# Weight tiles of a two-layer fp32 network placed by the address of the operand they meet, and one load moved to another queue

## The chip, the core and the metric

The kernel runs on one core of a Trainium2 chip. The metric is device time of one execution in microseconds (us). A core has TensorE (PE in the profile, with its weight loads shown apart as PEld), VectorE (DVE), ScalarE (ACT), GpSimd (POOL) and SyncE (SP), which here only issues DMAs. Operands lie in SBUF, 128 partitions side by side; an address below is the byte offset inside a partition.

## The reference

Two blocks of two layers each over x of 512 tokens by 1024 features, all in fp32, with a weight matrix behind nearly every step. Cut to its products:

```python
def first_block(x, c, ...):                      # i = 0: S5 state-space mixer, i = 1: short convolution
    for i in range(2):
        sh1, sc1, g1, sh2, sc2, g2 = split(silu(c) @ w_ada[i] + b_ada[i], 6)
        h = rms_norm(x, norm1_g[i]) * (1 + sc1) + sh1
        mix = s5_mixer(h, ...) if i == 0 else (bg * conv3(cg * v)) @ conv_w_out   # [bg, cg, v] = h @ conv_w_in
        x = x + g1 * mix
        h = rms_norm(x, norm2_g[i]) * (1 + sc2) + sh2
        g, u = split(h @ w_ffn_in[i], 2)
        x = x + g2 * ((silu(g) * u) @ w_ffn_out[i])
    return rms_norm(x, final_g)

def second_block(x, ...):                        # i = 0: dilated attention, i = 1: HGRN2
    for i in range(2):
        y = dilated_attention_mixer(x, ...) if i == 0 else hgrn2_mixer(x, ...)
        x = layer_norm(4 ** 0.25 * x + y, ln_mix_g[i], ln_mix_b[i])
        y = square(relu(x @ ffn_w_up[i])) @ ffn_w_down[i]
        x = layer_norm(4 ** 0.25 * x + y, ln_ffn_g[i], ln_ffn_b[i])
    return x
```

## The kernel before

**Products.** Activations are kept transposed, features on partitions and 512 tokens along the free axis. Each fp32 factor of a large product is split in two parts of type fp32r, a rounded one (`hi`) and the rest (`lo`), and a product is made of three: hi by hi, hi by lo, lo by hi. `mm` (L824 to L835) runs them for one block of 128 output features: for each of `nk` blocks of 128 input features three matmuls, L832, L833 and L834, whose stationary operand is a 128 by 128 piece of the weights (`whi`, `whi`, `wlo`) and whose moving operand is 512 or 256 columns of the activations (`hhi`, `hlo`, `hhi`). `mm_group` (L845 to L847) does the same for four output blocks at a time. The moving operands are `hhi`/`hlo` (the normalised input of a layer), `hidh`/`hidl` (its hidden values) and `ohi`/`olo` (the attention's output). Most products take 512 columns (`FULL`); where a layer's end waits on a norm, the tokens go in two halves of 256 (`HALF`). In a few products (the attention's and HGRN's `v`, L1205 and L1580, and the last product of all, L1734) the weights are the moving operand.

**Weights.** `load_raw` (L211) has SyncE load 1 MB of a weight matrix into one of three `raw` buffers. `split_w` (L781) takes a `whi` and a `wlo` buffer from the pool `wsp`, three of each, lets ScalarE write `whi` (L785) and VectorE `wlo` (L786). `load_centred` (L792) does so for matrices whose rows are made mean free. ScalarE may write a buffer again when TensorE has read it for the last time.

**Places.** In the built program the three `whi` and three `wlo` buffers are 8,192 bytes each, one behind the other, and start at 288 modulo 512. `hhi` and `hlo` start at 480 modulo 512, `hidh` and `hidl` at 288, but in the HGRN layer at 480; `ohi` and `olo` at 0. Every slice that a matmul reads starts a multiple of 512 bytes from its tile's start. By **distance** this text means the address of the weights of the next matmul less the address of the moving operand of the current one, modulo 512: it is 320 where `hhi` or `hlo` moves (288 - 480 + 512), 0 where `hidh` or `hidl` moves, but 320 in HGRN, and 288 where `ohi` or `olo` does.

**The start.** Ahead of these products stands the S5 mixer (`s5`, about the first 195 us), whose order is a list written by hand (`ORDER`), which a scheduler then lays out on each engine. ScalarE's queue issues constants, `brow`, `crow` and x in chunks (`xT`, L185, two DMAs of 1 MB in pieces of 512 bytes); SyncE's queue issues the small tables and then the adaptive-norm weights (`w_ada`, L232), 1 MB at a time. The chunks of x are first read by `token_scale` (L583). GpSimd builds the output tables `ft` (`out_tables`, L539 to L541).

Of the kernel before, what the change touches and what calls it, by code (L numbers as in the profile page):

```python
# [17 lines left out]
D = 1024  # L18
# [10 lines left out]
def make_consts():  # L29
# [30 lines left out]
    ct["selB"] = np.concatenate([(kj == 4 * (qi % 32) + r).astype(f) for r in range(4)], 1)  # L60
# [32 lines left out]
def body(ctx, tc, a, out):  # L93
# [100 lines left out]
    avg = const.tile([128, 128], F32, name="avg")  # L194
    P.memset(avg, 1.0 / D)
# [176 lines left out]
    def s5():  # L372
# [196 lines left out]
        def setup(_):  # L569

# [218 lines left out]
    def load(W, M, k0, nk, c0, ncol=256):  # L789
        return split_w(load_raw(W, k0, nk, c0, ncol, M), nk, ncol)  # L790

    def load_centred(W, M, k0, nk, nb, base=0):  # L792
# [20 lines left out]
    def centre(tag):  # L813
# [6 lines left out]
        T.matmul(mb, avg, z, start=True, stop=True)  # L820
# [30 lines left out]
    nxt, got = [], []  # L851

# [4 lines left out]
    def take(W, M, k0, nk, c0, ncol=256):  # L857
        return got.pop(0) if got else load(W, M, k0, nk, c0, ncol)
# [12 lines left out]
    def run(blocks, xh, xl, kx, nk, k0=0, first=0, halves=HALF, last=0, done=None):  # L871
# [9 lines left out]
        if last:  # L881
            ld = [load(W, M, k0, nk, c0) for W, M, c0, _ in blocks[end:]]
# [18 lines left out]
    def out_gemm(W, off, src, nkt, upd, done, centred=()):  # L901
# [5 lines left out]
        def part(c):  # L907
# [3 lines left out]
            if c in centred:  # L911
                ld = load_centred(W, D, k0, nk, 2)
                for m in range(0 if last else 8):
                    upd(m, mm(ld[m // 4], m % 4, xh, xl, kx, nk, FULL[0]), FULL[0], c, last)
            elif not last:
                for b in range(4):
                    w = load(W, D, k0, nk, b * 256)
                    for s in range(2):
                        upd(2 * b + s, mm(w, s, xh, xl, kx, nk, FULL[0]), FULL[0], c, last)
            else:  # L920
                ld = [load(W, D, k0, nk, b * 512, 512) for b in range(2)]
# [132 lines left out]
    def to_load(W, M, *cols):  # L1054
        nxt.extend([lambda c0=c0: load(W, M, 0, 8, c0) for c0 in cols])
# [72 lines left out]
    def qk_load(g, pr):  # L1128
# [15 lines left out]
    def upd_deep(ssum):  # L1144
        cnt = {}

        def upd(m, ps, ts, c, last):
# [7 lines left out]
            if last and ssum is not None:  # L1155
                accum_sq(ssum, m, ts, x)
# [11 lines left out]
    ap_ = at.enter_context(tc.tile_pool(name="at", bufs=2, reuse_waits="tile"))  # L1168
    load_consts(ap_, "m1", "selB", bufs=1)
# [22 lines left out]
    def v_items(g, b4):  # L1192
# [86 lines left out]
    def soft_steps(pr, steps, base):  # L1279
# [169 lines left out]
    got.append(load(Wa, DA, 0, 8, 2 * D))  # L1449
# [36 lines left out]
    w = load_centred(Wao, D, 6, 2, 1)[0]  # L1486
# [43 lines left out]
    hid_p = hg.enter_context(tc.tile_pool(name="hid3", bufs=1, reuse_waits="tile"))  # L1530
    inv_k = const.tile([128, 1], F32, name="inv_k")
# [21 lines left out]
    def hgrn_pair(b, first):  # L1553
# [20 lines left out]
        wv = load(Wh, 3 * D, 0, 8, 2 * D + b * 256)  # L1574
# [9 lines left out]
        for s in range(2):  # L1584
# [72 lines left out]
            for j in range(4):  # L1657
# [16 lines left out]
    psG = psum(mm=5, st=3)  # L1674
    part(1)
# [94 lines left out]
```

## Time and profile before

| | |
|---|---|
| three runs | 2798.68, 2799.27 and 2801.44 us, median 2799.27 |
| the profiled execution | 2796.92 us, its span 2795.1 us |
| TensorE busy | 2725.6 us, 98% of the span |
| VectorE, ScalarE, GpSimd busy | 56%, 38%, 5% |
| mean granted share of TensorE's clock | 0.992 |

A page of the profile gives busy times and the chain of work that ended last; groups of instructions give count and mean duration; a stretch gives each engine's busy time and count. A matmul's shown duration is longer than the distance between two starts, since matmuls overlap in TensorE's pipeline, so the pace is read from starts: the length of a stretch over the products that start in it.

### The profile page before, as it was taken

Reading aid. Unit: us, or ns where it says so; the run is one execution under the profiler, and the core shown is the slowest. Engines: PE = TensorE matmul, PEld = TensorE weight load, DVE = VectorE, ACT = ScalarE, POOL = GpSimd, SP = SyncE. Lnnn points to the kernel's source line nnn. Section 1 sums busy time; section 2 is a strip of 40 time slices with the busy share of each in tenths; the row PEclk is TensorE's granted clock in tenths of the full one; section 3 lists DMA queues with packets and bytes.
Section 4 is the critical chain, followed back from the end, with each engine's and each line's share of the span. In section 5 each row is a group of like instructions: output and inputs, shape, how many; then the busy total and the mean of one; then the engine's idle time right before and its main releaser. Section 6 shows DMA issues by size and latency. Waiting matters only on the chain.

```text
span 2795.1 us, 37486 instructions
## 1 busy us (share of the span) xinstructions
PE 2725.6 (98%) x15356; PEld 2282.9 (82%) x15356; DVE 1569.4 (56%) x2803; ACT 1068.5 (38%) x1874; POOL 127.2 (5%) x124
## 2 busy tenths in 40 slices
PE   5899999999999999999999999999999999999998
PEld 3568978889789888898888888898888988988887
DVE  7877755547545333375555555664446766744435
ACT  4653422224324222254343433452323666432322
POOL 6520000000000000000000000000000000000000
PEclk9889999999999999999999999999999999999999
DMA  8447445432333233343333333223224212223221
GB/s 220 145 133 223 151 137 177 143 124 83 121 106 99 83 98 97 97 128 88 98 89 88 96 84 91 69 87 95 91 83 128 81 61 66 86 91 102 87 83 61
DMA packets 300865, 298.37 MB, mean 107 GB/s; under 512 B 9733, under 2 KB 287109, under 8 KB 300693
## 3 DMA queue, kind: packets, MB, share of 16 engines
q1 hardware_dynamic: 288532, 277.27, 31.6%
q10 hardware_dynamic: 9824, 12.34, 2.0%
q0 software_dynamic: 2336, 6.36, 1.0%
q8 instruction: 121, 1.98, 0.3%
q14 instruction: 52, 0.42, 0.0%
HBM read 278.90 MB, written 2.10 MB: 101 GB/s over the span
## 4 chain that ended last, share of the span: by engine, by line
PE 90%; DVE 4%; ACT 3%; POOL 2%; issue 1%; ACTq 0%; DMA 0%; SPq 0%; DVEq 0%; POOLq 0%
PE ps_mm L832 24%; PE ps_mm L833 24%; PE ps_mm L834 24%; PE ps_mm L845 2%; PE ps_mm L846 2%; PE ps_mm L847 2%; PE ps_sc L1303 1%; PE ps_pt L1330 1%; PE ps_b L670 1%; POOL ft L541 1%; POOL ft L540 1%; PE ps_mm L1205 1%; PE ps_mm L1207 1%; PE ps_mm L1206 1%; PE ps_st L321 1%
## 5 line engine op out<-in xcount | busy, mean ns | idle before, releaser
L832 PE MATMUL ps_mm<-hhi,whi 128*128 128x512 f32 (+1 forms) x2064 | 795.3, 385 | 0.2 <-ACT silu L973 0.2
L833 PE MATMUL ps_mm<-hlo,whi 128*128 128x512 f32 (+1 forms) x2064 | 791.6, 384 | 0.4 <-DVE hlo L357 0.4
L834 PE MATMUL ps_mm<-hhi,wlo 128*128 128x512 f32 (+1 forms) x2064 | 790.0, 383 | 0.2 <-DVE wlo L786 0.2
L785 ACT CAST whi<-raw 128x1024 fp32r<-128x1024 f32 (+1 forms) x428 | 413.8, 990 | 835.8 <-PE ps_mm L833 652.5
L786 DVE TENSOR_TENSOR wlo<-raw,whi 128x1024 fp32r<-128x1024 f32 (+1 forms) x428 | 486.1, 1152 | 390.9 <-ACT whi L785 359.2
L832 PEld LDWEIGHTS ps_mm<-hhi,whi 128*128 128x128 f32 x2064 | 387.2, 188 | 84.9 <-issue 3.1
L834 PEld LDWEIGHTS ps_mm<-hhi,wlo 128*128 128x128 f32 x2064 | 387.2, 188 | 83.1 <-DVE wlo L786 0.6
L833 PEld LDWEIGHTS ps_mm<-hlo,whi 128*128 128x128 f32 x2064 | 387.7, 188 | 81.3 <-DVE hlo L357 0.9
L833 PE MATMUL ps_mm<-hidl,whi 128*128 128x512 f32 (+1 forms) x1120 | 402.2, 359 | 0.0
L832 PE MATMUL ps_mm<-hidh,whi 128*128 128x512 f32 (+1 forms) x1120 | 402.0, 359 | 0.0
L834 PE MATMUL ps_mm<-hidh,wlo 128*128 128x512 f32 (+1 forms) x1120 | 401.4, 359 | 0.0
L832 PEld LDWEIGHTS ps_mm<-hidh,whi 128*128 128x128 f32 x1120 | 211.1, 189 | 31.8 <-ACT hidh L356 0.2
L833 PEld LDWEIGHTS ps_mm<-hidl,whi 128*128 128x128 f32 x1120 | 211.2, 189 | 31.4
L834 PEld LDWEIGHTS ps_mm<-hidh,wlo 128*128 128x128 f32 x1120 | 211.2, 189 | 31.4
L1154 DVE TENSOR_TENSOR xT<-xT,ps_mm 128x512 f32<-128x512 f32 (+1 forms) x128 | 71.8, 569 | 121.2 <-PE ps_mm L834 120.3
L847 PE MATMUL ps_mm<-hlo,whi 128*128 128x256 f32 x448 | 123.9, 279 | 0.4 <-DVE hlo L357 0.4
L846 PE MATMUL ps_mm<-hhi,wlo 128*128 128x256 f32 x448 | 124.2, 279 | 0.0
L845 PE MATMUL ps_mm<-hhi,whi 128*128 128x256 f32 x448 | 123.3, 280 | 0.7 <-ACT hq L1559 0.6
L356 ACT CAST hidh<-silu 128x512 fp32r<-128x512 f32 (+1 forms) x124 | 68.9, 565 | 129.0 <-DVE silu L978 86.1
L939 DVE SCALAR_TENSOR_TENSOR xT<-ps_mm,mods,xT 128x512 f32<-128x512 f32 (+1 forms) x104 | 64.9, 626 | 93.6 <-PE ps_mm L834 93.2
L277 DVE SCALAR_TENSOR_TENSOR ada_acc<-raw,c_act,ada_acc 128x256 f32<-128x256 f32 x196 | 93.6, 484 | 4.9
L1254 POOL DMA_DIRECT2D qsw<-qc x48 | 23.4, 492 | 1582.8 <-ACT qc L1243 1568.6
(415 smaller groups left out, 3386.5 us busy)
## 6 DMA issues: line engine op xcount, KB each, us to landing
raw<-in_w_ada_dram SPq DMA_DIRECT2D x48, 1024.0 KB, 5.3
raw<-in_w_ffn_in_dram SPq DMA_DIRECT2D x44, 1024.0 KB, 5.2
raw<-in_ffn_w_up_dram SPq DMA_DIRECT2D x32, 1024.0 KB, 5.5
raw<-in_attn_w_in_dram SPq DMA_DIRECT2D x48, 512.0 KB, 5.1
raw<-in_ffn_w_down_dram SPq DMA_DIRECT2D x32, 768.0 KB, 4.4
raw<-in_w_ffn_out_dram SPq DMA_DIRECT2D x24, 768.0 KB, 4.5
raw<-in_conv_w_in_dram SPq DMA_DIRECT2D x12, 1024.0 KB, 5.3
raw<-in_attn_w_in_dram SPq DMA_DIRECT2D x12, 1024.0 KB, 5.0
```

The costliest lines, as they stand in the source:

```text
L277: V.scalar_tensor_tensor(ac, raw[:, k, :], c_act[:, k:k + 1], ac, op0=OP.mult, op1=OP.add)
L356: A.copy(hi, src)
L785: A.copy(hi[:, sl], raw[:, sl])
L786: V.tensor_tensor(lo[:, sl], raw[:, sl], hi[:, sl].bitcast(F32), op=OP.subtract)
L832: T.matmul(ps[:, 0:n], hi[:, k, cs], h, start=(k == 0), stop=False)
L833: T.matmul(ps[:, 0:n], hi[:, k, cs], l, start=False, stop=False)
L834: T.matmul(ps[:, 0:n], lo[:, k, cs], h, start=False, stop=(k == nk - 1))
L845: T.matmul(p[:, 0:n], hi[:, k, cs], h, start=(k == 0), stop=False)
L846: T.matmul(p[:, 0:n], lo[:, k, cs], h, start=False, stop=False)
L847: T.matmul(p[:, 0:n], hi[:, k, cs], l, start=False, stop=(k == nk - 1))
L939: V.scalar_tensor_tensor(x, ps, gcol[:, m:m + 1], x, op0=OP.mult, op1=OP.add)
L1154: V.tensor_tensor(x, x, ps, op=OP.add)
```

## The change

Six things change.

1. `w_tiles` is new. A weight buffer grows from 2,048 to 2,160 floats (8,192 to 8,640 bytes), and the tile is put at an offset inside it, so that it starts at a wanted place modulo 512. A counter that follows the pool's three buffers gives the offset. The place is `WIDE` (448) for weights that meet 512 columns and `NARROW` (256) for those that meet 256, plus a term for the operand that moves (`HID_LINE`, `HG_LINE`, `O_LINE`).
2. Three pads of 32 bytes are put in, so that the moving operands start at multiples of 64: in the built program `hhi`, `hlo`, `hidh` and `hidl` at 448 modulo 512, `hidh` and `hidl` of HGRN at 128, `ohi` and `olo` at 192.
3. The constant `avg` (128 by 128) goes; the centring product reads its stationary operand from one column, broadcast.
4. `selB` shrinks from 512 to 131 columns, read at shifted positions.
5. `rst` is loaded by a DMA of its own into the buffer of the norm sums, and the sums of HGRN's norm take that buffer later.
6. The two DMAs of x in chunks are issued by SyncE, from `setup`, behind the second load of `w_ada`.

With this the built program has, of 7,986 products of 512 columns that another follows, 7,975 at distance 0 (before: 2,401 at 0, 5,495 at 320, 90 at 288); of 3,891 with 256 columns, 3,122 at 320 and 760 at 192, the latter with the weights moving (before: 2,187 at 320, 762 at 0, 760 at 192, 182 at 288).

```diff
-    ct["selB"] = np.concatenate([(kj == 4 * (qi % 32) + r).astype(f) for r in range(4)], 1)
+    ct["selB"] = np.concatenate([np.zeros((128, 3), f), (kj == 4 * (qi % 32)).astype(f)], 1)
...
-    for s in range(2):
-        nc.scalar.dma_start(xc[64 * s:64 * s + 64].rearrange("p l i j -> p (l i) j"),
-                            dap(a["x"], s * 128, [[8 * D, 64], [256, 32], [1, 128]]))
+    def load_chunks():
+
+        for s in range(2):
+            nc.sync.dma_start(xc[64 * s:64 * s + 64].rearrange("p l i j -> p (l i) j"),
+                              dap(a["x"], s * 128, [[8 * D, 64], [256, 32], [1, 128]]))
...
+    const.tile([128, 8], F32, name="pad_c")
...
-    avg = const.tile([128, 128], F32, name="avg")
-    P.memset(avg, 1.0 / D)
...
         def setup(_):
+            load_chunks()
...
             hlo = hp_.tile([128, KT, S], R32, name="hlo")
+            hp_.tile([128, 8], F32, name="pad_h")
...
-    def split_w(raw, nk, ncol):
-        hi = wsp.tile([128, nk, ncol], R32, name="whi", tag="whi")
-        lo = wsp.tile([128, nk, ncol], R32, name="wlo", tag="wlo")
+    W_LINE, WIDE, NARROW, HID_LINE, HG_LINE, O_LINE = 320, 448, 256, 0, 192, 256
+    turn_of = [0]
+
+    def w_tiles(nk, ncol, place):
+        n = turn_of[0]
+        turn_of[0] = (n + 2) % 3
+        out = []
+        for i, nm in enumerate(("whi", "wlo")):
+            o = (place - W_LINE + 64 * (n + 3 * i)) % 512
+            assert o <= 448
+            t = wsp.tile([128, 2048 + 112], R32, name=nm, tag=nm)
+            out.append(t[:, o // 4:o // 4 + nk * ncol].rearrange("p (k c) -> p k c", k=nk))
+        return out
+
+    def split_w(raw, nk, ncol, place=WIDE):
+        hi, lo = w_tiles(nk, ncol, place)
...
-        T.matmul(mb, avg, z, start=True, stop=True)
+        T.matmul(mb, inv_d.to_broadcast([128, 128]), z, start=True, stop=True)
...
-        return got.pop(0) if got else load(W, M, k0, nk, c0, ncol)
+        return got.pop(0) if got else load(W, M, k0, nk, c0, ncol, NARROW)
...
             if c in centred:
-                ld = load_centred(W, D, k0, nk, 2)
+                ld = load_centred(W, D, k0, nk, 2, hid_line[0] + (NARROW if last else WIDE))
...
-                    w = load(W, D, k0, nk, b * 256)
+                    w = load(W, D, k0, nk, b * 256, 256, hid_line[0] + WIDE)
...
-    load_consts(hp, "tri", "rst", bufs=1)
+    load_consts(hp, "tri", "tri", bufs=1)
     tri = C("tri").bitcast(I32)
-    rst = C("rst")
+    rst = new_ssum()
+    o_rst, n_rst = CONST_OFF["rst"]
+    nc.scalar.dma_start(rst, a["consts"][:, o_rst:o_rst + n_rst])
```

SyncE's queue at the program's start, before. `raw` are the buffers of weights, `TT` tables of the S5 mixer.

```order
L173 DMA arow<-in_ssm_a_re_dram 64x64
L173 DMA arow<-in_ssm_a_im_dram 64x64
L174 DMA ls<-in_ssm_log_step_dram 64x1
L158 DMA vrow_82<-in_c_dram 8x128
L158 DMA vrow_82<-in_norm_g_dram 16x128
L158 DMA vrow_82<-in_b_ada_dram 96x128
L232 DMA raw<-in_w_ada_dram 128x8x256 x13
```

The same place now:

```order
L173 DMA arow<-in_ssm_a_re_dram 64x64
L173 DMA arow<-in_ssm_a_im_dram 64x64
L174 DMA ls<-in_ssm_log_step_dram 64x1
L158 DMA vrow_82<-in_c_dram 8x128
L158 DMA vrow_82<-in_norm_g_dram 16x128
L158 DMA vrow_82<-in_b_ada_dram 96x128
L234 DMA raw<-in_w_ada_dram 128x8x256 x2
L187 DMA xT<-in_x_dram 64x32x128 x2
L234 DMA raw<-in_w_ada_dram 128x8x256 x9
```

The two DMAs of x stand between the second and the third load of `w_ada`. ScalarE's queue from its last DMAs to its first computation, before (`vcol` are vectors turned to columns, `sn` a sine of the S5 poles, `c_act` the activated conditioning vector):

```order
L182 DMA crow<-in_ssm_c_re_dram 128x8x64
L182 DMA crow<-in_ssm_c_im_dram 128x8x64
L185 DMA xT<-in_x_dram 64x32x128 x2
L166 ACT_TABLE_LOAD
L166 COPY vcol_123<-ps_a 128x120
L431 ACT_TABLE_LOAD
L431 ACTIVATE sn<-t1y 128x64
L388 ACT_TABLE_LOAD
L388 ACTIVATE c_act<-vcol_123 128x8
```

and now:

```order
L182 DMA crow<-in_ssm_c_re_dram 128x8x64
L182 DMA crow<-in_ssm_c_im_dram 128x8x64
L166 ACT_TABLE_LOAD
L166 COPY vcol_120<-ps_a 128x120
L433 ACT_TABLE_LOAD
L433 ACTIVATE sn<-t1y 128x64
L390 ACT_TABLE_LOAD
L390 ACTIVATE c_act<-vcol_120 128x8
```

Nothing stands any more between the loads of `crow` and the first computation. Behind these rows the scheduler also orders the first 195 us anew on each engine (for example it puts the squares of x, L583, behind the tables of `io_matrices`); in the rest of the program the instructions on TensorE keep their order.

## Rows read from the trace of the kernel before

**Rows 1.** The page: span, busy time, the chain that ended last.

```profile
span 2795.1 us, 37486 instructions
PE 2725.6 (98%) x15356; PEld 2282.9 (82%) x15356; DVE 1569.4 (56%) x2803; ACT 1068.5 (38%) x1874; POOL 127.2 (5%) x124
...
PE 90%; DVE 4%; ACT 3%; POOL 2%; issue 1%; ACTq 0%; DMA 0%; SPq 0%; DVEq 0%; POOLq 0%
```

**Rows 2.** Waits: who waited for whom, us in total, times, longest.

```profile
ACT whi L785 <- PE ps_mm L833: 652.5, 145, 9.9
...
PE ps_a L553 <- DMA crow<-in_ssm_c_im_dram: 10.6, 1, 10.6
```

**Rows 3.** One stretch, after the S5 mixer: length, busy by engine (count), granted clock, DMA share, GB/s.

```profile
194.50:2795.10 2600.60, 2579.70 (x14269) 2179.33 (x14268) 1420.35 (x2548) 969.20 (x1652) 24.49 (x52) 1.00 0.33 103
```

**Rows 4.** TensorE's groups by shape: count, busy us, mean ns, idle before.

```profile
L833 PE MATMUL ps_mm<-hlo,whi 128*128 128x512 f32 x1840 | 729.3, 396 | 0.4 <-DVE hlo L357 0.4
...
L833 PE MATMUL ps_mm<-hidl,whi 128*128 128x512 f32 x800 | 311.9, 390 | 0.0
...
L833 PE MATMUL ps_mm<-hidl,whi 128*128 128x256 f32 x320 | 90.3, 283 | 0.0
...
L833 PE MATMUL ps_mm<-olo,whi 128*128 128x512 f32 x32 | 12.6, 395 | 0.0
```

**Rows 5.** Timeline: loads of the next weights beside the product that runs.

```profile
880.27 0.39 PE L833 MATMUL ps_mm<-hlo,whi 128*128 128x512 f32 x1
880.28 0.19 PEld L834 LDWEIGHTS ps_mm<-hhi,wlo 128*128 128x128 f32 x1
```

**Rows 6.** Stretches of unbroken products: length, PE busy (count), then as rows 3.

```profile
879.36:980.13 100.77, 100.77 (x434) 81.20 (x433) 33.34 (x37) 26.93 (x36) 0.00 (x0) 1.00 0.32 104
2078.21:2132.61 54.40, 54.40 (x241) 45.04 (x240) 29.35 (x35) 12.44 (x14) 0.00 (x0) 1.00 0.34 107
2391.56:2403.20 11.64, 11.64 (x51) 9.34 (x50) 6.57 (x10) 3.11 (x6) 0.00 (x0) 1.00 0.29 91
638.66:651.60 12.94, 12.94 (x109) 12.94 (x108) 9.42 (x18) 6.59 (x11) 0.00 (x0) 1.00 0.26 81
2436.88:2461.23 24.35, 24.35 (x217) 24.35 (x216) 15.60 (x35) 14.30 (x33) 0.00 (x0) 1.00 0.15 48
299.33:323.92 24.59, 24.59 (x211) 24.59 (x210) 18.65 (x37) 12.82 (x24) 0.00 (x0) 1.00 0.31 98
```

**Rows 7.** Timeline of the start: start, us, engine, line, operation [idle before <-releaser].

```profile
8.00 0.46 PE L164 MATMUL ps_a<-cst_ident,vrow 120*128 120x120 f32 x1
...
8.20 12.06 ACTq L185 DMA_DIRECT2D xT<-in_x_dram  x2
20.30 1.28 ACT L166 ACT_TABLE_LOAD   x1 [20.30 <-DMA crow<-in_ssm_c_im_dram]
21.02 1.35 PE L553 MATMUL ps_a<-cst_ident,crow 128*128 128x128 f32 x5 [10.59 <-DMA crow<-in_ssm_c_im_dram]
...
27.11 0.90 PE L553 MATMUL ps_a<-cst_ident,crow 128*128 128x128 f32 x3
...
29.22 1.27 ACT L554 ACTIVATE c<-ps_a,cst_sws 128x512 f32<-128x512 f32 x2
30.56 9.90 POOL L539 TENSOR_TENSOR ft<-c,pw_re 128x512 f32<-128x512 f32 x8 [5.37 <-DVE tq L424]
32.96 0.63 ACT L583 ACTIVATE ssq_t<-xT 128x512 f32<-128x512 f32 x1 [1.71 <-DMA xT<-in_x_dram]
...
74.51 1.97 POOL L540 TENSOR_TENSOR ft<-c,pw_im 128x512 f32<-128x512 f32 x1
```

**Rows 8.** Timeline of SyncE's queue around the third load of `w_ada`.

```profile
4.42 2.00 SPq L232 DMA_DIRECT2D raw<-in_w_ada_dram  x2
...
7.51 0.64 SPq L232 DMA_DIRECT2D raw<-in_w_ada_dram  x1
...
27.24 3.74 SPq L232 DMA_DIRECT2D raw<-in_w_ada_dram  x2
```

More of the change, by code (lines that the diff above doesn't have):

```diff
@@ L787, in split_w, with load, load_centred @@
         return hi, lo
-    def load(W, M, k0, nk, c0, ncol=256):
-        return split_w(load_raw(W, k0, nk, c0, ncol, M), nk, ncol)
-    def load_centred(W, M, k0, nk, nb, base=0):
+    def load(W, M, k0, nk, c0, ncol=256, place=WIDE):
+        return split_w(load_raw(W, k0, nk, c0, ncol, M), nk, ncol, place)
+    def load_centred(W, M, k0, nk, nb, place, base=0):
         n = D // nb
@@ L804, in load_centred @@
         for raw in raws:
-            hi = wsp.tile([128, nk, n], R32, name="whi", tag="whi")
-            lo = wsp.tile([128, nk, n], R32, name="wlo", tag="wlo")
+            hi, lo = w_tiles(nk, n, place)
             for k in range(nk):
@@ L851, in body @@
     nxt, got = [], []
+    hid_line = [HID_LINE]
     def ahead():
@@ L881, in run @@
         if last:
-            ld = [load(W, M, k0, nk, c0) for W, M, c0, _ in blocks[end:]]
+            ld = [load(W, M, k0, nk, c0, 256, NARROW) for W, M, c0, _ in blocks[end:]]
             pump(last)
@@ L920, in part @@
             else:
-                ld = [load(W, D, k0, nk, b * 512, 512) for b in range(2)]
+                ld = [load(W, D, k0, nk, b * 512, 512, hid_line[0] + NARROW) for b in range(2)]
             if last:
@@ L1054, in to_load @@
     def to_load(W, M, *cols):
-        nxt.extend([lambda c0=c0: load(W, M, 0, 8, c0) for c0 in cols])
+        nxt.extend([lambda c0=c0: load(W, M, 0, 8, c0, 256, NARROW) for c0 in cols])
     FH = a["w_ffn_out"].shape[1]
@@ L1126, in body, with qk_load @@
     DA = 3 * 3 * D
-    def qk_load(g, pr):
+    def qk_load(g, pr, place=WIDE):
         raw = raw_p.tile([128, 8, 256], F32, name="raw", tag="raw")
@@ L1132, in qk_load @@
                               dap(a["attn_w_in_2"], (3 * g + i) * D + pr * 128, [[DA, 128], [128 * DA, 8], [1, 128]]))
-        return split_w(raw, 8, 256)
-    nxt.extend([lambda g=g: qk_load(g, 0) for g in range(2)])
+        return split_w(raw, 8, 256, place)
+    nxt.extend([lambda g=g: qk_load(g, 0, NARROW) for g in range(2)])
     ffn(a["w_ffn_in"], D * 2 * FH, a["w_ffn_out"], FH * D, FH, True, upd_gate(mod(1, 5), ss3),
@@ L1155, in upd @@
             if last and ssum is not None:
-                accum_sq(ssum, m, ts, x)
+                accum_sq(ssum[0] if isinstance(ssum, list) else ssum, m, ts, x)
         return upd
@@ L1168, in body @@
     ap_ = at.enter_context(tc.tile_pool(name="at", bufs=2, reuse_waits="tile"))
+    ap_.tile([128, 8], F32, name="pad_a", bufs=1)
     load_consts(ap_, "m1", "selB", bufs=1)
@@ L1198, in go @@
                 if t == 0:
-                    box["w"] = got.pop(0) if got else load(Wa, DA, 0, 8, (3 * g + 2) * D + b4 * 256)
+                    box["w"] = got.pop(0) if got else load(Wa, DA, 0, 8, (3 * g + 2) * D + b4 * 256, 256, NARROW)
                     vv[g, b4] = ap_.tile([128, 4, 256], F32, name="v", bufs=3)
@@ L1385, in joint2 @@
             for r in range(4):
-                T.matmul(pf, C("selB")[:, 128 * r:128 * r + 128], fm[:, r], start=(r == 0), stop=(r == 3))
+                T.matmul(pf, C("selB")[:, 3 - r:131 - r], fm[:, r], start=(r == 0), stop=(r == 3))
             f1 = sm8("jf1")
@@ L1429, in go @@
                 if m == 0:
-                    w = load_centred(Wao, D, 2 * b4, 2, 1)[0]
+                    w = load_centred(Wao, D, 2 * b4, 2, 1, O_LINE + (NARROW if ts in HALF else WIDE))[0]
                     box["w"] = att["w", b4] = w
@@ L1448, in body @@
     ws = [(got.pop(0), 2, first_qk(g)) for g in range(2)]
-    got.append(load(Wa, DA, 0, 8, 2 * D))
+    got.append(load(Wa, DA, 0, 8, 2 * D, 256, NARROW))
     first_blocks(ws)
@@ L1674, in body @@
     psG = psum(mm=5, st=3)
+    zs2.append(new_ssum())
     part(1)
@@ L1724, in last_part @@
     def last_part(W, k0, nk, hi, lo):
-        ld = [load(W, D, k0, nk, b * 512, 512) for b in range(2)]
+        ld = [load(W, D, k0, nk, b * 512, 512, hid_line[0] + WIDE) for b in range(2)]
         xr = residuals()
```

10 lines of the change are left out of this document (6 added, 4 removed).

## The prediction, made before the changed kernel ran

> **What bounds the kernel now.** I read the page first. TensorE is busy for 98% of the span and is 90% of the chain that ended last [rows 1]. The waits say which way the pressure goes: ScalarE stood 652.5 us waiting for TensorE to give back a weight buffer [rows 2], so weights are ready before they are wanted. After the S5 mixer, TensorE is busy in 2579.7 of 2600.6 us at a granted clock of 1.00, VectorE in 1420 and ScalarE in 969 [rows 3]. Nothing there is to be gained from waits. What is left is the pace at which one product follows another.
>
> That pace is read from stretches in which nothing but these products runs. Each stretch of [rows 6] goes from the first start to the start after the last one; from its count come off the one or two products whose tails reach in. With `hhi`/`hlo` moving, 512 columns: 432 products in 100.77 us, **233.3 ns**. With `hidh`/`hidl` moving, the same 512 columns, the same granted clock: 240 in 54.40 us, **226.7 ns**. With 256 columns it is the other way round: `hid` 108 in 12.94 us, 119.8 ns; `hhi` 215 in 24.35 us, 113.3 ns, and in another stretch 209 in 24.59 us, 117.7 ns. [...] The groups by shape say the same over all products: 396 ns shown for L833 with `hlo`, 390 with `hidl` [rows 4].
>
> What differs between the two is not the loop (the same three lines) nor the tile's kind: in HGRN, where `hidh`/`hidl` lie at 480 modulo 512 instead of 288, 50 products of 512 columns take 11.64 us, 233 ns, the pace of `hhi`, in the third stretch of [rows 6]. The weights lie at 288 throughout. So the pace goes with the places. While a product streams, the next one's weights are loaded, from the same moment on (880.27 and 880.28) [rows 5]: two reads of SBUF run side by side, and their distance modulo 512 is 320 in the slow case of 512 columns and 0 in the fast one; for 256 columns 320 is the fast one.
>
> [...]
>
> **The change part by part.** The sum is made against the profiled execution, 2796.9 us, which is 2.4 us under the median of 2799.3.
>
> *Products of 512 columns.* 3 × 1,840 with `hhi`/`hlo` [rows 4], and by the code 96 in HGRN and 96 with `ohi`/`olo` of like pace, 5,712 in all, go from distance 320 (or 288) to 0. Taken at 233.3 - 226.7 = 6.6 ns each this is 37.7 us. About 3 in 100 start behind a transpose, a norm or a late operand, and their gap is no stream's: 36.5 us. From the shown durations (396 against 390) it would be 34. I take **36**. The 2,304 of `hid` in the feed-forward and convolution layers stay at distance 0.
>
> *Products of 256 columns.* 3 × 320 with `hid` less HGRN's 192, 768, go from distance 0 to 320: from 119.8 ns to 113.3 or 117.7, whichever the stream falls into. Halfway, 115.5, is 4.3 ns, 3.3 us; the 192 with `ohi`/`olo` gain perhaps half a microsecond more. I take **4** (bounds 1.6 and 5.5). Those with `hhi` keep their distance.
>
> *The places themselves.* No row has both operands at a multiple of 64. The nearest is distance 0 at 288 and 288, at 32 modulo 64 both, and I take its 226.7 for the new one, because the relation of the two is the same. [...]
>
> *Who could be late next.* Products that take 1.6% less time ask for weights 1.6% sooner. VectorE has 45% and ScalarE 63% of the main stretch free [rows 3], DMA 67%: nothing becomes late.
>
> *The start.* ScalarE issues the two DMAs of x for 12.06 us, and only then does its first work, at 20.30, though what it copies was ready at 8.46 [rows 7]. Without them it is free 11.8 us sooner. The next thing late is `crow`: TensorE waited 10.6 us for it until 21.02 [rows 2, 7], which the move does not touch. Its eight transposes are 1.35 + 0.90 us and the two copies of `c` 1.27, so `c` is there at about 24.5 instead of 30.49, and GpSimd, which starts on `ft` at 30.56 and then is busy without a break until 76, starts 6 us sooner. On SyncE the 12 us stand ahead of the third load of `w_ada` (7.51) and of the fourth, which waited for a buffer until 27.24 [rows 8]: the queue was idle between. x itself is issued at 6.4 instead of 8.2, behind two loads of 1 MB, and was first waited for at 32.96. Then follow 110 us in which VectorE, TensorE and ScalarE take turns in an order that the scheduler has made anew. I take **5 us** saved; bounds +5 (the new order loses as much) and -11.8 (all that ScalarE gains).
>
> *The rest.* The fill of `avg` (GpSimd, at the start) is hidden or gone; the broadcast column feeds three centrings; `selB` feeds the same products. The DMA of `rst` is one more issue on ScalarE, under 0.5 us; it waits until the norm sums are read, which ScalarE's next instruction behind it waits for too, and HGRN's first scan comes tens of us later. I count +0.4.
>
> **Sum:** 2796.9 - 36 - 4 - 5 + 0.4 = 2752.3; with the 2.4 up to the median, **2755 us**.
>
> **The rivals.**
>
> *One step more.* [...] Chance 0.16.
>
> *The places count for nothing.* Something else that `hhi` and HGRN's `hid` share makes their pace, and only the start gains: 2799.3 - 5 + 0.4 = 2795, within 0.2% of before (2793.7 to 2804.9; about what a measurement of this kernel can tell from no change). Against it: HGRN's `hid` runs the same lines in the same form as the other layers'. The same time would come if the buffers did not get the places wanted; the built program's addresses speak against that. Chance 0.07.
>
> *Slower: the moving operand's own place decides, not the distance.* 288 is then the good place for 512 columns, 480 and 0 bad ones, and all move to 448, which is nearest to 480. Then nothing is won at 512, `hid` loses 6.6 ns on 2,304 products, +15.1, and gains 3.3 at 256; with the start: 2799.3 + 15.1 - 3.8 - 5 + 0.4 = 2806. It decides from the point where 448 behaves as 480. For it: at 512 columns no row has the moving operand at 288 with a distance other than 0. Against it: `ohi`, at 0, and `hhi`, at 480, run alike though their places have nothing in common, while both have a distance other than 0. Chance 0.06.
>
> *Half the gain.* The new places save only part of the step, or the start loses 5: 2766 to 2790. Chance 0.09.
>
> **How the numbers follow.** The forecast, 2740 to 2765, has 0.62. Faster by over 0.2%: 0.62 + 0.16 + 0.09 = 0.87; within 0.2%: 0.07; slower: 0.06. The range takes in the step more and half the gain, 2700 to 2790, and leaves out the two cases in which the places win nothing.
>
> **What would show it.** Right: in the profile after, unbroken products of 512 columns start 226.7 ns apart under `hhi` and `hid` alike, L832 to L834 show about 390 ns with `hhi`, and those of 256 with `hid` 113 to 118. The S5 mixer ends some 5 us sooner, ScalarE's first work stands near 9 us and GpSimd's first `ft` near 24.5. [...] The places count for nothing if `hhi` stays at 233.3; the moving operand's place decides if `hid` rises to it. The start is wrong if x or a load of `w_ada` is waited for. What would upset the whole is a pace at 512 columns above 233.3, or VectorE or ScalarE named as what TensorE waits for after 195 us.

## The result, and the profile after

| | before | after |
|---|---|---|
| median of the runs beside each other | 2798.97 us (4 runs) | 2767.34 us (4 runs, 2764.64 to 2769.32) |
| ratio, 95% interval | | 0.9885 [0.9868, 0.9902] |
| the profiled execution, its span | 2796.92, 2795.1 us | 2767.48, 2765.7 us |
| first product of the main part starts | 194.56 us | 195.84 us |

The kernel is 1.15% faster: 2767.3 where 2755 was predicted, inside the range of 2700 to 2790, 2 us above the forecast's own 2740 to 2765. The page of the changed kernel, beside [rows 1]:

```profile
span 2765.7 us, 37495 instructions
...
PE 2694.6 (97%) x15356; PEld 2286.1 (83%) x15356; DVE 1565.3 (57%) x2803; ACT 1068.6 (39%) x1874; POOL 123.5 (4%) x123
...
PE 90%; DVE 4%; ACT 3%; DMA 1%; POOL 1%; issue 1%; SPq 0%; DVEq 0%; ACTq 0%; POOLq 0%
```

TensorE is still the bound and has 31 us less to do. Now the stretches that answer to [rows 3] and [rows 6] (length, PE busy with its count, PEld, DVE, ACT, POOL, granted clock, DMA share, GB/s):

```profile
195.80:2765.70 2569.90, 2549.39 (x14269) 2183.27 (x14268) 1419.32 (x2548) 969.10 (x1652) 24.51 (x52) 1.00 0.33 104
870.74:968.68 97.94, 97.94 (x434) 81.08 (x433) 33.08 (x37) 26.89 (x36) 0.00 (x0) 1.00 0.32 107
2055.30:2109.70 54.40, 54.40 (x241) 45.06 (x240) 29.25 (x35) 12.45 (x14) 0.00 (x0) 1.00 0.34 107
2366.65:2377.78 11.13, 11.13 (x51) 9.20 (x49) 6.57 (x10) 3.09 (x5) 0.00 (x0) 1.00 0.31 96
631.89:644.61 12.72, 12.72 (x110) 12.72 (x108) 9.38 (x18) 6.61 (x11) 0.00 (x0) 1.00 0.25 82
2411.78:2436.03 24.25, 24.25 (x216) 24.25 (x215) 15.49 (x35) 14.19 (x33) 0.00 (x0) 1.00 0.13 45
665.80:690.65 24.85, 24.85 (x214) 24.85 (x212) 19.29 (x42) 12.48 (x23) 0.00 (x0) 1.00 0.26 87
```

The same 14,269 products from the first one on take 2549.4 us instead of 2579.7. The second row is `hhi` with 512 columns, 432 products (two of the count are tails) in 97.94 us, 226.7 ns, where it was 233.3. The third is `hid`, 240 in 54.40, 226.7, as before. The fourth is HGRN's `hid`, 49 in 11.13, 227.1 where it was 233. The last three have 256 columns: `hid` 108 in 12.72, 117.8 ns; `hhi` 214 in 24.25, 113.3; `hhi` again 211 in 24.85, 117.8.

The groups by shape, as [rows 4] (count, busy us, mean ns, idle before):

```profile
L850 PE MATMUL ps_mm<-hlo,whi 128*128 128x512 f32 x1840 | 720.0, 391 | 0.5 <-DVE hlo L359 0.5
...
L850 PE MATMUL ps_mm<-hidl,whi 128*128 128x512 f32 x800 | 311.6, 389 | 0.0
...
L850 PE MATMUL ps_mm<-hidl,whi 128*128 128x256 f32 x320 | 89.9, 282 | 0.0
```

`hlo` has come down from 396 ns to 391, beside `hidl` at 389; `hidl` with 256 columns stands at 282 after 283. Nothing new waits in the main part: ScalarE still stands for TensorE to give weight buffers back, 628.8 us in all after 652.5 [rows 2]:

```profile
ACT whi L803 <- PE ps_mm L850: 628.8, 143, 9.8
```

Counted over every pair of neighbouring products in the two profiled executions (the distance from one start to the next, waits included), the terms of the prediction's sum come out so:

| term | predicted | measured | from |
|---|---|---|---|
| 512 columns, 7,986 pairs | -36 | -33.2 | 1860.2 to 1827.0 us |
| 256 columns, 3,891 pairs | -4 | +2.3 | 462.0 to 464.3 us |
| the start, to the first product | -5 | +1.3 | 194.56 to 195.84 us |
| `rst`, and what is left | +0.4 | +0.2 | main part 30.7 shorter in all |
| sum | -44.6 | -29.4 | 2796.9 to 2767.5 us |

Three questions follow: is it the distance that sets the pace, why did 256 columns win nothing, and where did the start lose what ScalarE gained?

### The profile page after: what moved, and what is told of

It reads as the page before. It is cut to its first block, busy times and chain, and to the rows that moved or that the text cites. A ratio compares the mean times of both kernels' runs of the same rounds, so it can differ in the third digit from the quotient of the medians.

```text
span 2765.7 us, 37495 instructions
## 1 busy us (share of the span) xinstructions
PE 2694.6 (97%) x15356; PEld 2286.1 (83%) x15356; DVE 1565.3 (57%) x2803; ACT 1068.6 (39%) x1874; POOL 123.5 (4%) x123
## 4 chain that ended last, share of the span: by engine, by line
PE 90%; DVE 4%; ACT 3%; DMA 1%; POOL 1%; issue 1%; SPq 0%; DVEq 0%; ACTq 0%; POOLq 0%
PE ps_mm L849 24%; PE ps_mm L850 24%; PE ps_mm L851 24%; PE ps_mm L862 2%; PE ps_mm L863 2%; PE ps_mm L864 2%; PE ps_sc L1322 1%; PE ps_pt L1349 1%; PE ps_b L673 1%; PE ps_mm L1224 1%; ACT whi L803 1%; POOL ft L543 1%; PE ps_mm L1226 1%; PE ps_x L241 1%; PE ps_mm L1225 1%
## 5 line engine op out<-in xcount | busy, mean ns | idle before, releaser
L849 PE MATMUL ps_mm<-hhi,whi 128*128 128x512 f32 (+1 forms) x2064 | 786.5, 381 | 0.0
L850 PE MATMUL ps_mm<-hlo,whi 128*128 128x512 f32 (+1 forms) x2064 | 782.6, 379 | 0.5 <-DVE hlo L359 0.5
L851 PE MATMUL ps_mm<-hhi,wlo 128*128 128x512 f32 (+1 forms) x2064 | 781.2, 378 | 0.5 <-DVE wlo L804 0.5
L803 ACT CAST whi<-raw 128x1024 fp32r<-128x1024 f32 (+1 forms) x428 | 414.0, 990 | 819.5 <-PE ps_mm L850 628.8
```

The lines of the kernel that those rows point to most:

```text
L803: A.copy(hi[:, sl], raw[:, sl])
L849: T.matmul(ps[:, 0:n], hi[:, k, cs], h, start=(k == 0), stop=False)
L850: T.matmul(ps[:, 0:n], hi[:, k, cs], l, start=False, stop=False)
L851: T.matmul(ps[:, 0:n], lo[:, k, cs], h, start=False, stop=(k == nk - 1))
```

## Experiments on the places

**All eight multiples of 64 in one kernel.** In `w_tiles` of the changed kernel:

```diff
+        place = place + 64 * (block_of[0] % 8)
+        block_of[0] += 1
```

> The changed kernel, but every block of weights is put 64 bytes further from its wanted place than the block before it, so that the distance between the next weights and the moving operand goes through all eight multiples of 64 modulo 512, at 512 and at 256 columns, while hhi stays at 448, hid at 448 (HGRN 128). Distance theory: at 512 columns 226.7 ns at distance 0 and 233.3 ns at 320, under hhi and hid alike; if 0 is the only good one, 7 of 8 products lose 6.6 ns and the time is about 2813 us, if 320 is the only bad one about 2774. Rival (the moving operand's own place decides, 448 being a good one): 226.7 ns at every distance, about 2767. Rival (the places count for nothing): the same pace at every distance. At 256 columns the distance theory wants 119.8 ns at 0 and 113.3 or 117.8 at 320; that one of the others always gives 113.3 is possible and nothing before this run says so.

2799.88 us, one execution. Eight blocks one behind the other, `hhi` moving from 448 throughout, 48 products each (a count of 49 or 50 has tails in it); the distances are 128, 192, 256, 320, 384, 448, 0 and 64:

```profile
891.07:902.22 11.15, 11.15 (x49) 9.04 (x48) 3.65 (x4) 3.12 (x4) 0.00 (x0) 1.00 0.28 96
902.22:913.21 10.99, 10.99 (x49) 9.01 (x48) 3.83 (x4) 3.10 (x4) 0.00 (x0) 1.00 0.29 95
913.21:924.09 10.88, 10.88 (x49) 9.01 (x48) 3.65 (x4) 3.11 (x4) 0.00 (x0) 1.00 0.29 96
924.09:935.29 11.20, 11.20 (x50) 9.02 (x48) 3.83 (x4) 3.10 (x4) 0.00 (x0) 1.00 0.23 72
935.29:946.44 11.15, 11.15 (x49) 9.05 (x48) 3.65 (x4) 3.11 (x4) 0.00 (x0) 1.00 0.22 71
946.44:957.44 11.00, 11.00 (x49) 9.02 (x48) 3.83 (x4) 3.10 (x4) 0.00 (x0) 1.00 0.22 71
957.44:968.35 10.91, 10.91 (x50) 9.01 (x48) 3.12 (x4) 2.69 (x4) 0.00 (x0) 1.00 0.23 74
968.35:979.54 11.19, 11.19 (x49) 9.02 (x48) 3.21 (x4) 2.67 (x4) 0.00 (x0) 1.00 0.29 94
```

Divided by 48: 232.3, 229.0, 226.7, 233.3, 232.3, 229.2, 227.3, 233.1 ns. The pace changes from block to block with the weights' place alone, and it repeats after 256 bytes. Nothing else differs between these blocks; the rivals that the places count for nothing, and that the moving operand's own place decides, both fall. A third rival, that the weights' own place decides, falls by the kernel before: there the weights lay at 288 throughout and ran at 226.7 ns under `hid`, at 288, and at 233.3 under `hhi`, at 480 [rows 6]. So the distance sets the pace. That 0 is not the only good distance is why the time is 2800 and not 2813.

**Distances of 16 to 240 bytes.** The same with steps of (16, 32, 48, 80, 96, 160, 224, 240) modulo 256.

> The changed kernel with the blocks of weights put, one after the other, at distances of 16, 32, 48, 80, 96, 160, 224 and 240 bytes modulo 256, at both column counts. The first scan gave 227.4, 233.2, 232.4 and 229.3 ns for 512 columns at 0, 64, 128 and 192 modulo 256. If the pace follows the distance byte by byte, 16, 32, 224 and 240 lie between their neighbours or below them, and one of them may be a step of 6.67 ns under 227; if it follows 64 byte lines that both reads touch, all distances that are no multiple of 64 share the pace of the slow neighbours, about 232 to 233. For 256 columns (119.8, 113.3 or 117.8, 118.5, 117 ns at 0, 64, 128, 192) the question is whether a distance between 32 and 96 gives 113.3 in every stream.

2808.60 us, one execution. `hid` at distance 272 (16 modulo 256), then at 288 (32), 36 products each:

```profile
624.76:632.92 8.16, 8.16 (x37) 6.76 (x36) 3.86 (x4) 2.00 (x2) 0.00 (x0) 1.00 0.39 128
...
1903.29:1911.68 8.39, 8.39 (x37) 6.76 (x36) 3.20 (x4) 1.57 (x2) 0.00 (x0) 1.00 0.43 133
```

226.7 and 233.1 ns. Over all pairs of both scans (59 to 853 in each group, once pairs over 260 ns are left out), the means for 512 columns are:

| distance modulo 256 | `hhi`, `hlo`, ns | `hidh`, `hidl`, ns |
|---|---|---|
| 240 | 227.6 | 226.8 to 226.9 |
| 0 | 227.3 to 227.6 | 227.4 to 227.5 |
| 16 | 229.0 to 229.3 | 226.7 |
| 32, 48, 64 | 233.1 to 233.3 | 233.1 to 233.3 |
| 80 | 231.9 to 232.0 | 232.0 to 232.3 |
| 96 | 234.1 to 234.3 | 234.0 to 234.2 |
| 128 | 232.4 to 232.5 | 232.2 to 232.3 |
| 160 | 233.3 to 233.4 | 233.1 to 233.8 |
| 192 | 229.3 to 229.5 | 229.2 to 229.3 |
| 224 | 233.1 to 233.2 | 233.2 to 233.3 |

Good, modulo 256, are 240 and 0. At 16 `hid` runs at its best, 226.7, but `hhi` at 229, no better than at 192; why the two differ there, though both start at 448, is open. No distance goes under 226.7, so the rival of one step more (a pace as far below 226.7 as that is below 233.3) falls for every place tried. For 256 columns no distance gave 113.3 in every stream: the means are 119 to 120 at 0, 117.5 to 120 at 128, and 117 to 120 at those of the fine scan, and at the odd multiples of 64 most streams have 113.3 or 117.8.

**Without the pads.** Three lines of padding out, the places moved along: everything 32 bytes off a multiple of 64, the distances as in the changed kernel (but for the products with `ohi`, of which 88 with 512 columns lie at 32).

```diff
-    W_LINE, WIDE, NARROW, HID_LINE, HG_LINE, O_LINE = 320, 448, 256, 0, 192, 256
+    W_LINE, WIDE, NARROW, HID_LINE, HG_LINE, O_LINE = 288, 480, 288, -64, 128, 192
```

> The changed kernel without the three pads of 32 bytes: moving operands and weights all lie 32 bytes off a multiple of 64 (hhi 480, hid 416, HGRN's hid 96), the weights moved along so that the distances stay 0 at 512 columns and 320 at 256. Distance theory: 226.7 ns at 512 columns as in the changed kernel, 2767 us. Rival (the alignment to 64 makes the pace): 233.3 ns again, +53 us, about 2800 at most with the other terms.

2768.76 us (4 runs), ratio 0.9881 [0.9864, 0.9899]: the changed kernel's. `hhi` from 480, 431 products:

```profile
870.37:968.09 97.72, 97.72 (x434) 80.92 (x432) 33.34 (x37) 26.94 (x36) 0.00 (x0) 1.00 0.33 107
```

226.7 ns. `hhi` at 480 was slow before, 233.3, and is fast here, at the changed kernel's pace with 448, 226.7: at 512 columns the alignment to 64 made no difference.

Together the scans show paces from 226.7 to 234.3 ns that go with the distance of two of TensorE's own reads.

## Experiments on 256 columns

**What a stream does.** In the changed kernel's trace a stream of 256 columns at distance 320 held one pace over many products, after a pause some took the other, and one did so after one late product (near 2172 us the steps from start to start go from 113 ns by a single one of 135 to 118): `hhi` at 2411.78 ran 214 products at 113.3, at 665.80 it ran 211 at 117.8. In the kernel before, the stream that answers to the latter ran at 113.3. The third `hhi` stream of the program (near 299 us) came out at 113.4 in 6 of 12 executions, and at 117.8 in the other 6, at one and the same distance. The five first streams of `hid`, which go on from 512 columns without a pause, are another matter: in eight executions with distance 0 ahead of them all 40 began at 117.8. Nor is every stream behind a pause drawn anew: 64 products of `hhi` near 282 us had 117.8 in all 12 executions. And 211 of `hhi` near 1813 us had 113.4 in the three executions with `hhi` at 480 (the kernel before, the same with x on SyncE, and the one without pads) and 117.8 in the nine with `hhi` at 448, at distance 320 in all 12; so at 256 columns the place itself may count, which no run here tests.

**Another distance ahead.** On the kernel with x on ScalarE (below), the last block of `hid` products of 512 columns goes to 320 (in `load_centred` likewise). It stands straight ahead of four of these five streams. Ahead of the other one (near 2140 us) stand products of `hhi`, which the edit leaves at 0.

```diff
-                    w = load(W, D, k0, nk, b * 256, 256, hid_line[0] + WIDE)
+                    w = load(W, D, k0, nk, b * 256, 256, hid_line[0] + (NARROW if b == 3 and c == nch - 2 else WIDE))
```

> The kernel of the run with x on ScalarE, and of each series of hid products the last block of 512 columns ahead of the 256 column ones is put at distance 320 instead of 0. So far a stream of 256 column products that goes on from one of 512 without a pause ran at 117.8 ns behind distance 0 and at 113.4 behind 64 or 320 (first scan; HGRN of the kernel before). If the pace of such a stream is set by the product in front of it, the five first streams of hid (108 products each) come to 113.4: 5 x 108 x 4.4 ns = 2.4 us won, 1 us lost on the blocks that now run at 233.2, time about 1.4 us under that run's 2764.8. If it falls by chance, some of the five stay at 117.8 and nothing or a loss of 1 us is seen.

2767.80 us (4 runs), ratio 0.9889 [0.9874, 0.9903]. The expectation misread the first scan: the two streams at 113.5 and 113.8 there lay at 64 and 320 themselves, behind 192 and 448, and the one behind 64 ran at 117.8. The first of the five, and HGRN's (107 products without tails):

```profile
638.50:651.22 12.72, 12.72 (x110) 12.72 (x108) 9.39 (x18) 6.58 (x11) 0.00 (x0) 1.00 0.26 82
2385.67:2397.85 12.18, 12.18 (x109) 12.18 (x107) 8.14 (x17) 6.06 (x10) 0.00 (x0) 1.00 0.28 87
```

117.8 and 113.8 ns. HGRN's stream changed; the three others that the edit reached began at 117.8 as ever, and so did the one that it did not reach. The product in front is thus not what decides alone, and the theory falls in three cases of four. The same came out in the next run. HGRN's stream by itself went with the distance ahead: 113.4 to 113.8 in four executions behind 320, 117.8 in eight behind 0. What decides stays open.

**The turned products** (weights moving) at distance 320 too:

```diff
-        wv = load(Wh, 3 * D, 0, 8, 2 * D + b * 256, 256, NARROW)
+        wv = load(Wh, 3 * D, 0, 8, 2 * D + b * 256, 256, TURNED)
```

(and at the attention's two loads; `TURNED` is 128).

> The run with the last block at distance 320, and the products in which the weights are the moving operand (256 columns, 760 of them) put at distance 320 instead of 192. In every trace so far these ran at 117.8 ns at 192; the one stream of the first scan at 320 ran at 113.3. If 320 gives 113.3 to all of them, 760 x 4.4 ns = 3.4 us are won on top: about 2760. If the pace is set where the stream begins and falls either way, about half of it.

2767.82 us (4 runs), ratio 0.9884 [0.9868, 0.9901]: no change in time. Of eight streams four came to 113.3 to 113.7 and four stood at 117.8. The mean over all pairs is 115.7 ns, against 117.2 to 117.8 at 192 in five executions, which is 1.1 to 1.6 us. Against what was expected, not all had run at 117.8 at 192: the first of the eight ran at 113.4 in the kernel before, and stands at 117.8 here. The same four did so in the run with x split and this place (below), from which these two rows are:

```profile
1336.22:1346.80 10.58, 10.58 (x95) 10.58 (x95) 5.56 (x17) 3.68 (x12) 0.17 (x1) 1.00 0.56 150
2225.10:2236.30 11.20, 11.20 (x97) 11.20 (x95) 7.31 (x12) 11.10 (x16) 0.00 (x0) 1.00 0.27 93
```

## Experiments on the start

The rows that answer to [rows 7]: ScalarE's first work, GpSimd's first `ft`, the w_ada products (L241) and those that TensorE's queue has ahead of the third block of them, the end of GpSimd's first block of `ft` (where `sr` begins), the second gains (L608), the first product of the main part (timeline: start, us, engine, line, operation [idle before <-releaser]):

```profile
8.46 1.28 ACT L166 ACT_TABLE_LOAD   x1 [8.46 <-DMA cst_sws<-in_consts_dram]
...
22.30 2.41 POOL L541 TENSOR_TENSOR ft<-c,pw_re 128x512 f32<-128x512 f32 x2 [4.48 <-ACT c L556]
...
34.09 3.75 PE L567 MATMUL ps_b<-b,cst_e 128*128 128x512 f32 x4 [3.34 <-DVE b L426]
42.50 3.73 PE L528 MATMUL ps_c<-IC,w 128*128 128x144 f32 x14 [4.67 <-DVE w L426]
46.16 1.22 PE L241 MATMUL ps_x<-raw,cz 128*32 128x256 f32 x16
...
66.43 4.02 POOL L625 TENSOR_TENSOR sr<-w8p,cst_sws 128x512 f32<-128x512 f32 x2
...
81.62 0.43 PE L608 MATMUL ps_a<-mv,cst_e 128*128 128x64 f32 x2
...
195.84 0.50 PE L849 MATMUL ps_mm<-hhi,whi 128*128 128x512 f32 x1
```

and, of the kernel before, the rows of the third w_ada block, the second gains, the end of GpSimd's block and the first product:

```profile
33.13 1.93 PE L239 MATMUL ps_x<-raw,cz 128*32 128x256 f32 x16
...
72.21 0.43 PE L605 MATMUL ps_a<-mv,cst_e 128*128 128x64 f32 x2 [1.59 <-DVE mv L424]
...
76.44 3.04 POOL L622 TENSOR_TENSOR sr<-w8p,cst_sws 128x512 f32<-128x512 f32 x2
...
194.56 0.50 PE L832 MATMUL ps_mm<-hhi,whi 128*128 128x512 f32 x1
```

ScalarE began 11.8 us sooner, GpSimd 8.3, and its block ended 10.0 sooner. But TensorE's queue now has the third block of w_ada behind products that wait for VectorE, and took it at 46.16 instead of 33.13. The second gains, which need eight such blocks, came at 81.62 instead of 72.21, and the lead was gone.

**The move undone, and the move alone.** The changed kernel with x on ScalarE's queue again:

```diff
-            nc.sync.dma_start(xc[64 * s:64 * s + 64].rearrange("p l i j -> p (l i) j"),
+        nc.scalar.dma_start(xc[64 * s:64 * s + 64].rearrange("p l i j -> p (l i) j"),
```

> The changed kernel with the two DMAs of x back on ScalarE's queue, ahead of its first computation. If moving them cost what the two traces show (first product of the main part at 195.84 us against 194.57), the time is 1 to 2 us under the changed kernel's 2767.3: 2766. If the move did save the 5 us that the prediction put down for it, and something else in the change gave them back in the first 195 us, the first product comes 5 us later and the time is about 2772.

2764.80 us (4 runs), ratio 0.9865 [0.9844, 0.9887], first product at 194.88. And the kernel before with only x moved to SyncE (the same line the other way round, called from `setup`):

> The kernel before with only the two DMAs of x moved to SyncE, behind the second load of w_ada. The prediction's term for this is -5 us (bounds -11.8 and +5): 2794. By the two traces the move lets ScalarE and GpSimd begin 8 to 12 us sooner and then loses it all to loads of w_ada that are asked for later: then 2800, with GpSimd's last ft of the first block near 66 us instead of 76 and the first product of the main part near 195.8.

2802.28 us (10 runs) against 2799.93 (13 runs), ratio 1.0007 [0.9998, 1.0016]; `sr` at 66.52, first product at 196.07. So the move alone gains nothing. Nor is a gain from undoing it shown: the 2.5 us of the first of these runs were not seen again in the two kernels above that also have x on ScalarE (2767.8 both, of which their blocks at 320 cost 1.2 by the pairs). With the next runs the table is:

| x issued by | first product, one execution each, us | medians, us |
|---|---|---|
| ScalarE (new places) | 194.88, 201.47, 195.73 | 2764.8, 2767.8, 2767.8 |
| SyncE, behind two loads of w_ada | 195.84, 196.77, 195.79, 196.15, 195.43 | 2767.3, -, -, 2768.8, 2766.6 |
| SyncE, behind three | 199.33 | 2766.6 |
| GpSimd | 203.66 | 2775.3 |
| one by ScalarE, one by SyncE | 196.56, 188.92 | 2762.1, 2762.3 |

**Behind the third load:**

```diff
-    ORDER = ("A1 A1 K0 A1 A1 B0 T2 Q0 ...
+    ORDER = ("A1 A1 A1 K0 A1 B0 T2 Q0 ...
```

> The changed kernel with the third load of w_ada ahead of the two DMAs of x on SyncE. If the start lost its gain because TensorE's queue takes the third block of w_ada products behind the products that wait for VectorE (46.2 us, where before it came at 33.1), this puts it back ahead of them: the second part of the gains comes sooner, the first product of the main part lies several us under 195.84, near 190, and the time near 2762. If the S5 chain has another limit behind that (GpSimd's ft, the scans on VectorE), the first product stays at 194 to 196 and the time at 2765 to 2768.

2766.63 us (4 runs), ratio 0.9880 [0.9865, 0.9895]. The third block of w_ada came at 29.72, but the fourth only at 49.64: the hole had moved by one block. No gain.

**On GpSimd:** `nc.gpsimd.dma_start` in the same place.

> The changed kernel with the two DMAs of x issued by GpSimd, which stood idle from 7.2 to 15.9 us. SyncE then has no x in front of w_ada, and ScalarE none in front of its first work: if those two queues are all that matters, the first product of the main part comes 5 us or more sooner, near 190, time near 2762. If issuing a MB in pieces of 512 bytes costs GpSimd as much as the 12 us that it costs ScalarE, it delays c_act's copy and the first ft, and the first product stays near 195, time 2766.

2775.28 us (4 runs), ratio 0.9915 [0.9898, 0.9931], 8 us slower than the changed kernel. TensorE had six blocks of w_ada begun by 46.16, so those were not late; GpSimd was:

```profile
2.13 2.20 POOL L187 DMA_DIRECT2D xT<-in_x_dram  x2
...
18.38 0.20 POOL L227 COPY cz<-c_act 128x8 f32<-128x8 f32 x1 [14.05 <-ACT ab L434]
18.51 0.95 POOL L574 MEMSET X<- 128x1024 f32 x1
19.40 1.80 POOL L579 MEMSET TT<- 128x2048 f32 x1
21.25 2.34 POOL L575 TENSOR_TENSOR X<-drow,cst_e 16x1024 f32<-16x1024 f32 x1
23.55 1.79 POOL L579 MEMSET TT<- 128x2048 f32 x1
28.00 1.10 POOL L541 TENSOR_TENSOR ft<-c,pw_re 128x512 f32<-128x512 f32 x1 [2.66 <-ACT c L556]
```

The two DMAs took 2.2 us to issue, not 12, but with them the scheduler put the fills of `X` and `TT` behind the copy to `cz`, in front of `ft`.

**One DMA on each queue**, ScalarE's ahead of its first work, SyncE's behind three loads of w_ada:

```diff
+    load_chunk(0, nc.scalar)
...
-            load_chunks()
+            load_chunk(1, nc.sync)
```

> The changed kernel with one DMA of x on ScalarE, as before, and the other on SyncE behind the third load of w_ada. In the order that comes of it TensorE takes the w_ada blocks ahead of the products that wait for VectorE, as in the kernel before, and ScalarE waits for one DMA of x instead of two. If the late w_ada blocks are what took back the gain at the start, the first product of the main part comes clearly under 194.5, at about 190, time near 2762. If the first part of the program is bound elsewhere by then, it stays at 194 to 196: 2766 to 2768.

2762.10 us (4 runs, 2757.90 to 2767.09), ratio 0.9864 [0.9849, 0.9879]; in the profiled execution, its slowest, the first product stands at 196.56. With the turned products at 320 added:

> The run with x split over ScalarE and SyncE, with the turned products at distance 320 as well. If both gains hold (x split 2762.1 against 2767.3; three of the six turned streams at 113.3, 1.6 us), about 2760.5. If the lead of the split was chance between executions, whose first 200 us have differed by up to 6.6 us with the same instructions in the same order, it stands level with the changed kernel beside it, at 2765 to 2767.

2762.29 us (4 runs, 2761.04 to 2766.69), ratio 0.9866 [0.9851, 0.9881], first product at 188.92. And the changed kernel beside it:

> The changed kernel as it is, once more on the chip of the run beside it: 2767 again, with its first product of the main part at 195.8 to 196.2, and its 256 column streams falling to 113.3 and 117.8 otherwise than in its first profile behind pauses, but at 117.8 again in the five first streams of hid.

2766.63 us (4 runs), ratio 0.9884 [0.9868, 0.9901]. Over eight runs each the split has a median of 2762.3, the changed kernel 2766.9. It is the fastest version here, by some 4.6 us, though the intervals of the ratios still overlap, and four of its eight runs have the turned products at 320, worth 1.1 to 1.6 us.

The two executions of the split show what a single profile of the start is worth. The two programs have the same instructions in the same order on every engine and do not differ in their first 180 us, and yet the first products lie 7.6 us apart. TensorE's rows and two stretches of the execution at 196.56:

```profile
73.81 0.88 PE L673 MATMUL ps_b<-U,bt 128*128 128x64 f32 x6
81.30 4.18 PE L528 MATMUL ps_c<-IC,w 128*128 128x144 f32 x16 [6.61 <-DVE X L426]
...
85.99 5.79 PE L673 MATMUL ps_b<-U,bt 128*128 128x64 f32 x26
```

```profile
80.00:85.00 5.00, 3.70 (x15) 3.73 (x16) 5.00 (x8) 1.51 (x4) 2.02 (x1) 0.50 0.00 0
85.00:90.00 5.00, 5.00 (x26) 5.00 (x25) 4.98 (x8) 4.49 (x9) 0.00 (x0) 0.50 0.13 34
```

and of the one at 188.92:

```profile
80.25 0.88 PE L673 MATMUL ps_b<-U,bt 128*128 128x64 f32 x6
80.97 2.18 PE L528 MATMUL ps_c<-IC,w 128*128 128x144 f32 x16
...
83.35 3.09 PE L673 MATMUL ps_b<-U,bt 128*128 128x64 f32 x26
```

```profile
70.00:75.00 5.00, 5.00 (x31) 3.25 (x31) 4.10 (x4) 2.39 (x9) 5.00 (x4) 0.50 0.35 96
75.00:80.00 5.00, 5.00 (x32) 3.85 (x30) 2.25 (x6) 2.20 (x7) 2.36 (x2) 0.64 0.33 117
80.00:85.00 5.00, 5.00 (x47) 4.75 (x42) 5.00 (x9) 4.27 (x12) 1.47 (x1) 1.00 0.66 210
85.00:90.00 5.00, 4.68 (x46) 3.98 (x46) 5.00 (x8) 4.88 (x10) 0.00 (x0) 1.00 0.34 92
```

In the one TensorE stood idle for 6.61 us and came back at a granted clock of 0.50: the 26 products with `U` took 5.79 us. In the other it had no such gap, the clock was 1.00 from 80 to 90 us, and the same 26 took 3.09. That one had not been spared the lower clock: it had it earlier, at 0.50 from 70 to 75 us, and came to the first 6 products with `U` 6.4 us later (80.25 for 73.81). But that cost it nothing, since the next products, with `IC`, started at about the same time in both (80.97 and 81.30). The 7.6 us come about behind that: the products with `rb` (L692) start at 105.61 in the one and at 98.26 in the other. From 40 to 80 us the mean granted clock was 0.82 in the first and 0.70 in the second, from 80 to 120 us 0.75 and 0.96. What differs is where the lower clock fell, not whether it came.

## Why the prediction was right, and where it was wrong

*Right: what bounds, and the distance.* The main part was paced by products, and the pace went with the distance: `hhi` and HGRN's `hid` came to 226.7 and 227.1, `hid` stayed, and the two scans and the kernel without pads show that it is the distance. Taking the value at 288 and 288 for the new places held: 226.7 under `hid`, 227.2 under `hhi`.

*512 columns: -33.2 for -36, mis-sized.* The step was put at 6.6 ns for all but 3 in 100. Over the 5,300 undisturbed pairs with `hhi` and `hlo` the mean went from 233.30 to 227.23, 6.07 ns: a part of them sits at 230 to 236, and 0.56 ns on 5,300 are 3.0 us. Why these few do is not shown.

*256 columns: +2.3 for -4, the step that failed.* The prediction took a stream at 320 for one that falls to 113.3 or 117.7, halfway, and counted only the products whose distance changed. Those of `hid` outside HGRN gained 2.1 us (92.0 to 89.9), not 3.3, since their first streams began at 117.8 in all eight executions with distance 0 ahead. What it left out is that streams whose distance did not change took the other pace as well: `hhi` lost 2.2 (235.0 to 237.2), HGRN's `hid` 0.7, the turned ones 0.4; and those with `ohi`, which it put at a gain of 0.5, lost 0.9, pauses included. In the second profile of the changed kernel the 256 columns come to 461.9 us, 0.1 under before. Over the seven executions here that have the new places, blocks at 320 and turned products apart, they come to 461.2 to 464.3, 462.8 in the mean; over the two with the old places to 462.0 and 464.2. So no gain is shown, where 4 was forecast.

*The start: +1.3 for -5, the step that failed.* Its first links held: ScalarE at 8.46 (near 9 expected), GpSimd's `ft` at 22.30 (near 24.5). The step that broke is "the queue was idle between": SyncE was, but with x in front the scheduler laid w_ada's products later into TensorE's queue, behind waits for VectorE, and the prediction named a sign near this one ("a load of `w_ada` is waited for"). What TensorE waited for ahead of them was VectorE, 3.34 and 4.67 us in the rows above, and not a load: the third was issued at 16.58, and loads of `w_ada` landed within 14 us. The order of the two kernels was at hand and showed it. Its size can't be read from one profile: executions of one order differ by up to 7.6 us here, and only the medians say that the move is worth nothing. That w_ada's lateness costs the lead is read from the rows and fits the split, where w_ada and ScalarE are both early and some 3 to 4.6 us come back; it is not shown, since a run that changed TensorE's order alone was not made, and what the lower clock took in each execution was not set apart.

*The rivals.* One step more, places that count for nothing and the moving operand's own place are refuted by the scans (in the last, 2,304 products at 6.6 ns are 15.2 us, not 15.1). The range's lower end, 2700, takes in a gain of one step more, 53 us, that no run shows: the lowest pace of 512 columns at any distance was 226.7 ns. The time fell outside the forecast's own range and at the near edge of "half the gain", which had 0.09, but for a reason that it only half names: the places gave 33 of 36, and it was the start and the 256 columns that gave nothing.

## What to carry to other kernels

Where TensorE is the bound and products follow one another without a pause, read the pace from starts, stretch by stretch, and sort the pairs by the address of the next weights less that of the moving operand: here 0 instead of 64, modulo 256, was worth 6 ns of 233, and a scan with one distance for each block of weights answers for many places in one run. A DMA that is taken off one queue can be paid for elsewhere: ask which products or tables the scheduler now lays behind it, and compare the order before trusting the gain. What is worth a few microseconds at a start with pauses is judged by medians of several runs, not by one profile.

## What was not expected of the hardware

The pace of 512 columns repeated with the distance after 256 bytes, not 512 (232.3 ns at 128 and at 384), and was not a matter of equal or unequal alone: 226.7 to 227.6 at 240 and 0, 229.3 at 192, 232 at 80 and 128, 234 at 96.

Most streams of 256 columns at an odd multiple of 64 showed one of two paces, 113.3 and 117.8 ns, and one held its pace for 214 products. Both came at one distance and in one program; what chooses is open, beyond this: behind a pause some streams changed from execution to execution (near 299 us 6 of 12 had 113.4) and others did not (near 282 us 12 of 12 had 117.8), and without a pause it repeated in every execution of one arrangement (40 of 40 first streams of `hid`).

In one execution with x split, TensorE stood idle in the start for 6.61 us, until 81.30, and the granted clock was 0.50 in every stretch of 5 us from 80 to 95 us, after 1.00 from 70 to 75. In an execution of the same instructions the stretch at 0.50 fell earlier (70 to 75 us), the products with `IC` started at 80.97 without such a wait, and the first product of the main part came 7.6 us sooner.
